# A gate in front of the second weight pool of a mixture of experts: its first load waits for a GpSimd memset that is queued behind the first gather

## The chip, the cores and the metric

The kernel runs on one core of a Trainium2 chip. The metric is the device time of one execution in microseconds. Before the change it is 1295.51 us, the median of 3 runs (1295.21 to 1295.92). A core has the engines PE (matmuls), DVE (vector), ACT (scalar), POOL (GpSimd) and SP (which issues most DMAs here), each with an instruction stream of its own that it works off in the order of the program.

## The reference

One decoder layer over 1024 tokens of 1024 values in float32: a token mixer (sliding-window attention beside a spatial gate), a cross-attention to 256 memory tokens, and a mixture of experts. The change lies in the last one:

```python
p_group = softmax(xf @ w_router_group); g_idx = argmax(p_group)            # one of 4 groups
local = take(xf @ w_router_expert, g_idx); top_logit, top_idx = top_k(local, 2)   # two of its 8 experts
gate = softmax(top_logit) * p_group[g_idx]
# for each of the 32 experts e, over the tokens that chose it:
hid = silu(xblk @ w1[e]) * (xblk @ w3[e])
y[token] += gate * (hid @ w2[e])
```

## The kernel before

The dense part (mixer, cross-attention) runs to about 676 us. The last half of the tokens is then routed (`route`, a chain of small DVE, POOL and PE work that ends in the table `idx`), and the rest of the span is the expert stage.

In the expert stage `main` runs 32 rounds, one for each expert, in the order 0, 8, 16, 24, 1, 9 and so on. For a round:

- POOL gathers up to 96 token rows of the normalised residual `xd` from DRAM into a tile `X` (an indirect DMA, `gather`, L1021). There are two `X` tiles; the first two gathers are issued ahead of the first round, the gather of round i+2 in round i.
- `columns` (L1038) turns `X` by eight PE transposes and splits it into `xh` (ACT) and `xl` (DVE): matmuls run in a rounded float32 format, three for each product (L114, L115, L116).
- The weights of an expert come in 12 tiles `ew` of 128x1024, 0.5 MB each, four for each of `w1`, `w3`, `w2`. Each tile is used in two halves: ACT casts a half to `hi` (L1049), DVE makes `lo` = weight - `hi` (L1050). `hi` and `lo` have five buffers each, so ACT can be five casts ahead of PE.
- `hidden`: 48 matmuls into two `h`; ACT's `g` (silu, L1066) and DVE's `g` follow. `turn`: four PE transposes of `g`, split into `hh` (ACT) and `hlo` (DVE). `output`: 24 matmuls into two `y`; ACT writes them to `B`, scaled by the gate (L1090, two instructions). Round i does the `output` of expert i-1.
- POOL adds `B` into the output rows in DRAM (`scatter`, L1027).

The weight tiles come from two pools, `raw` with 19 and `more` with 18 buffers, in turn: tiles 0 to 18 in `raw`, 19 to 36 in `more`, 37 again in `raw`. `stream` (L989) allocates a tile and issues its load on SP's queue (L998). The first 24 tiles (two experts) are streamed ahead: 19 while the dense part ends, since `raw` lies in memory that is free by then, and the last five by `run_all(units)` at L1336, as soon as the dense part's pools are closed and `more` exists. From the third expert on, a round's tiles are loaded from within `main`. A load waits for the buffer that it overwrites (DVE's `lo` of the tile that was in it).

In round 20 `counts` computes on DVE, between the weights' instructions, how many experts have more than 96 tokens (`cnt`, `no`, `noc`, `noi`); every engine reads `noi` into a register (L1164), SP in the midst of its loads.

The order in which each engine gets its instructions is not the order of the code: a scheduler sets it when the program is built, from priorities and its own estimate of times. It also decides which buffer a tile gets.

Of the kernel before, what the change touches and what calls it, by code (L numbers as in the profile page):

```python
# [821 lines left out]
class Moe:  # L822
# [166 lines left out]
    def stream(self, r, src):  # L989

        for i in range(3):
            r.append([])
            for u in range(4):
                k = self.turns % (self.nraw + self.nmore)
                self.turns += 1
                pool, n = ("raw", self.nraw) if k < self.nraw else ("more", self.nmore)
                w = self.L[pool].tile([P, 1024], F32, name="ew", bufs=n)
                self.nc.sync.dma_start(w, src(i, slice(u * 1024, (u + 1) * 1024)))  # L998
                r[i].append(w)
                yield  # L1000
# [91 lines left out]
    def order(self):  # L1092
        return [g * 8 + j for j in range(8) for g in range(4)]

    def main(self, xd, out, pre, rest):


        idx, tb, n = self.idx, self.tb, self.cap
        order = self.order()
        ix = lambda i: idx[:n, order[i]:order[i] + 1]  # L1100
        touch = []

        def ordered(ins, i):
            for j, o in touch:
                if order[j] // 8 != order[i] // 8:
                    self.tc.declare_no_dep(ins.ins, o.ins, reason="rows of tokens of another group")
            touch.append((i, ins))

        X, B = (lambda i: self.X[i % len(self.X)]), (lambda i: self.B[i % len(self.B)])
        get = lambda i: self.gather(X(i)[:n], ix(i), xd)  # L1110
        for i in range(len(self.X)):
            get(i)
        xc = self.columns(X(0), n)
        prev = None
        turned = []

        def between():
            run_all(rest)
            if prev:
                turned.append(self.turn(prev[3], n))  # L1120

        def finish():
            i, e, w, g = prev
            b = B(i)
            self.output(w, turned.pop() if turned else self.turn(g, n), b, tb[:, 0, e:e + 1], n)
            ordered(self.scatter(b[:n], ix(i), out), i)

        for i in range(NE):
            if i == 20:
                self.counts()  # L1130
            e = order[i]
            w = pre.pop(e) if e in pre else self.expert(e)
            if i + len(self.X) < NE:
                get(i + len(self.X))
            with self.tc.issue_after(self.ready.ins) if i == 0 else nullcontext():
                g = self.hidden(w, xc, tb[:, 1, e:e + 1], n, between)
            if i + 1 < NE:
                xc = self.columns(X(i + 1), n)
            if prev:
                finish()  # L1140
            prev = (i, e, w, g)
        finish()
# [80 lines left out]
def run_all(*gens):  # L1223
    for g in gens:
        for _ in g:
            pass


def to_tail(g):
    while next(g) != "tail":  # L1230
        pass


def interleave(a, b, ra, rb):

    live = [a, b]
    while live:
        for g, n in ((a, ra), (b, rb)):
            for _ in range(n):
                if g in live and next(g, live) is live:  # L1240
                    live.remove(g)


def dense(m):
    run_all(m.gate(0), m.gate(1))
    kv = m.kv()
    next(kv)
    interleave(kv, m.mix_tokens(), 1, 1)
    run_all(m.u(0), m.u(1))


def build(tc, a, dbg=None, cap=96):
    nc = tc.nc
    L = {}
    with ExitStack() as top:
        def pool(stack, name, **kw):
            L[name] = stack.enter_context(tc.tile_pool(name=name, bufs=1, reuse_waits="tile", **kw))

        pool(top, "const", side="left")
        L["dram"] = top.enter_context(tc.tile_pool(name="dram", bufs=1, space=DRAM))  # L1260
        xd = L["dram"].tile([T, D], F32, name="xd")
        m = Pre(tc, a, L, xd)
        m.rs2 = L["const"].tile([P, 8], F32, name="rs2")
        m.logit = L["const"].tile([P, 8, 36], F32, name="logit")
        m.setup()
        moe = Moe(tc, a, L, m, cap)
        moe.turns, moe.nraw, moe.nmore, moe.nhl = 0, 19, 18, 5
        pre = ExitStack()
        mix = ExitStack()
        for n in ("act", "ring", "half", "tmp"):  # L1270
            pool(pre, n, side="left")
        for n in ("early", "q2", "mem", "mix", "rt0"):
            pool(mix, n, side="right")
        pool(pre, "pt", side="left")
        pool(pre, "ps", space=PSUM)
        m.start(0, lambda: m.load(PIECES["q"][0], 0, 1))
        q = m.q()
        next(q)
        m.setup_mixer()
        interleave(q, m.x_stats(0), 1, 1)  # L1280
        run_all(m.mem_stats())
        m.use_stats()
        moe.consts()
        m.router_weights()
        dense(m)
        m.q_norm()
        mem = m.memory()
        at = m.attn()
        interleave(mem, at, 1, 1)
        run_all(mem)  # L1290
        run_all(m.x_stats(1))
        run_all(m.out_proj())
        x = m.cross()
        to_tail(x)
        m.start(1)
        m.use_stats()
        q = m.q()
        interleave(x, q, 1, 1)
        dense(m)
        m.q_norm()  # L1300
        co = m.co_proj(0)
        at = m.attn()
        interleave(at, co, 2, 1)
        run_all(co)
        interleave(m.out_proj(), chain([0], m.co_tail(0), moe.route(0)), 1, 1)
        x = m.cross()
        to_tail(x)
        next(x)
        co = m.co_proj(1, lambda: run_all(x))
        next(co)  # L1310
        next(co)
        mix.close()
        pool(top, "rt1", side="right")
        pool(top, "raw", side="right")
        pool(pre, "st", side="right")
        order = moe.order()
        ahead = {e: [] for e in order[:2]}
        units = chain(*(moe.ahead(e, r) for e, r in ahead.items()))
        for _ in range(6):
            next(units)  # L1320
        early = islice(units, moe.nraw - 6)
        interleave(co, early, 1, 1)
        run_all(co, early, m.co_tail(1))
        ro = moe.route(1)
        next(ro)
        next(ro)
        next(ro)
        if dbg == "size":
            for n, p in L.items():
                print(n, getattr(p, "current_size", lambda: 0)() / P)  # L1330
            return
        pre.close()
        for n in ("more", "ov", "rows", "ew", "hl"):
            pool(top, n, side="left")
        pool(top, "ps", space=PSUM)
        run_all(units)  # L1336
        moe.rows()
        moe.main(xd, a["out"], ahead, ro)
        moe.overflow(xd, a["out"])
        if dbg == "size2":  # L1340
            for n in L:
                print(n, getattr(L[n], "current_size", lambda: 0)() / P)
            return
        if dbg:
            dbg(nc, a, m, moe, xd)
# [69 lines left out]
```

## Time and profile before

| | |
|---|---|
| median of the runs | 1295.51 us |
| the profiled execution | 1300.52 us, its span 1298.8 us |
| busy shares of the span | PE 94%, DVE 77%, ACT 70%, POOL 15% |
| moved by DMA | 317.95 MB, mean 245 GB/s; SP's and ACT's queue 283.04 MB |
| mean granted clock of PE | 0.974 |
| what ACT's and DVE's work on `ew` waits for, whole span | ACT's casts 35.9 us (DVE), PE 12.2 us (ACT); no row names a load |

The profiled execution is 0.4% above the median of the others. Busy shares are means over stages with different limits, so the stretches are read one by one below. In the tables of stretches the number in brackets is the count of instructions, and the clock is the share of full speed that was granted.

### The profile page before, as it was taken

The page shows a single profiled execution, that of the slowest core. Times are in us where ns is not written, and L with a number is a line of the kernel's source. Part 1 is how long each engine was busy: PE and PEld are TensorE (multiplying, and loading weights), DVE is VectorE, ACT ScalarE, POOL GpSimd, SP SyncE. Part 2 cuts the span into 40 slices and gives each one's busy share as a digit, 9 for nine tenths or more (in the row PEclk, how much of TensorE's full clock was granted, in tenths as well). Part 3 has the DMA queues.
Part 4 walks back from the last instruction along what each step waited for, and adds up shares of the span by engine and source line. Part 5 has one row for each costly group of instructions (what it writes and reads, how often), then busy time and mean ns, then how long its engine had stood idle before and what let it go on. Part 6 is the DMA issues. An engine that isn't in the chain of part 4 may idle for free.

```text
span 1298.8 us, 19994 instructions
## 1 busy us (share of the span) xinstructions
PE 1226.2 (94%) x6514; PEld 963.0 (74%) x6514; DVE 1006.2 (77%) x1991; ACT 904.7 (70%) x1739; POOL 190.6 (15%) x229
## 2 busy tenths in 40 slices
PE   7999889998999998999994999999999999999995
PEld 5998878887899777788773677777777777766663
DVE  6568886556365999646546899999999999988884
ACT  6559663444366774444433999999999999988884
POOL 1312220011120112110004111111111111111100
PEclk9999999998999999999996999999999999999998
DMA  8436555335423345633599889999999959999981
GB/s 282 152 108 205 174 181 195 122 115 171 136 85 117 93 138 163 225 100 113 186 342 364 289 297 383 391 380 380 372 383 374 381 166 364 380 390 384 390 307 15
DMA packets 114603, 317.95 MB, mean 245 GB/s; under 512 B 13760, under 2 KB 33344, under 8 KB 114496
## 3 DMA queue, kind: packets, MB, share of 16 engines
q1 hardware_dynamic: 95280, 283.04, 60.2%
q0 software_dynamic: 10624, 29.38, 9.0%
q10 hardware_dynamic: 8592, 4.23, 1.1%
q8 instruction: 52, 0.85, 0.3%
q14 instruction: 55, 0.45, 0.1%
HBM read 293.52 MB, written 31.46 MB: 250 GB/s over the span
## 4 chain that ended last, share of the span: by engine, by line
issue 42%; PE 35%; DVE 9%; POOL 8%; ACT 3%; DMA 3%; POOLq 0%; SPq 0%; DVEq 0%; ACTq 0%
PE mm L114 8%; PE mm L116 8%; PE mm L115 8%; POOL out_dram L1027 3%; POOL X L1021 2%; DVE wlo L99 1%; DMA raw<-in_wp_dram 1%; DVE S L491 1%; PE sc L114 1%; PE sc L115 1%; PE tp L193 1%; PE sc L116 1%; DVE S L474 1%; DVE ptl L107 1%; PE av L114 1%
## 5 line engine op out<-in xcount | busy, mean ns | idle before, releaser
L1050 DVE TENSOR_TENSOR lo<-ew,hi 128x512 fp32r<-128x512 f32 x768 | 477.7, 685 | 37.8 <-ACT hi L1049 35.9
L1049 ACT CAST hi<-ew 128x512 fp32r<-128x512 f32 x768 | 446.1, 621 | 32.8 <-PE h L116 7.0
L115 PE MATMUL h<-lo,xh 128*96 128x512 f32 x512 | 204.2, 399 | 2.7 <-DVE lo L1050 2.6
L114 PE MATMUL h<-hi,xh 128*96 128x512 f32 x512 | 205.3, 401 | 0.2 <-ACT xh L106 0.2
L116 PE MATMUL h<-hi,xl 128*96 128x512 f32 x512 | 203.6, 398 | 0.3 <-DVE xl L107 0.3
L114 PE MATMUL mm<-ah,whi 128*128 128x512 f32 x416 | 166.7, 402 | 12.1 <-ACT whi L98 7.4
L98 ACT CAST whi<-raw 128x1024 fp32r<-128x1024 f32 x92 | 96.1, 1047 | 112.0 <-PE mm L115 54.4
L116 PE MATMUL mm<-ah,wlo 128*128 128x512 f32 x416 | 164.9, 396 | 0.6 <-DVE wlo L99 0.5
L115 PE MATMUL mm<-al,whi 128*128 128x512 f32 x416 | 164.9, 396 | 0.5 <-DVE al L107 0.5
L99 DVE TENSOR_TENSOR wlo<-raw,whi 128x1024 fp32r<-128x1024 f32 x92 | 112.7, 1226 | 66.9 <-ACT whi L98 66.9
L114 PE MATMUL mm<-whi,ah 128*128 128x256 f32 x448 | 129.1, 289 | 3.5 <-ACT t8b L409 2.1
L115 PE MATMUL mm<-wlo,ah 128*128 128x256 f32 x448 | 128.1, 287 | 0.0
L116 PE MATMUL mm<-whi,al 128*128 128x256 f32 x448 | 128.0, 286 | 0.0
L115 PEld LDWEIGHTS h<-lo,xh 128*96 128x96 f32 x512 | 83.5, 163 | 41.3 <-DVE lo L1050 6.9
L114 PEld LDWEIGHTS h<-hi,xh 128*96 128x96 f32 x512 | 83.4, 163 | 38.2 <-ACT hi L1049 4.9
L116 PEld LDWEIGHTS h<-hi,xl 128*96 128x96 f32 x512 | 83.4, 163 | 34.5 <-DVE xl L107 1.0
L114 PE MATMUL y<-hi,hh 128*96 128x512 f32 x256 | 100.3, 398 | 1.4 <-ACT hh L106 1.4
L115 PE MATMUL y<-lo,hh 128*96 128x512 f32 x256 | 101.0, 395 | 0.2 <-DVE lo L1050 0.2
L116 PE MATMUL y<-hi,hlo 128*96 128x512 f32 x256 | 100.5, 393 | 0.0
L114 PEld LDWEIGHTS mm<-ah,whi 128*128 128x128 f32 x416 | 79.0, 190 | 27.7 <-ACT whi L98 7.9
L116 PEld LDWEIGHTS mm<-ah,wlo 128*128 128x128 f32 x416 | 79.0, 190 | 17.7 <-DVE wlo L99 1.7
L115 PEld LDWEIGHTS mm<-al,whi 128*128 128x128 f32 x416 | 79.1, 190 | 16.0 <-DVE al L107 1.1
(315 smaller groups left out, 2077.1 us busy)
## 6 DMA issues: line engine op xcount, KB each, us to landing
ew<-in_wm_dram SPq DMA_DIRECT2D x384, 512.0 KB, 11.6
raw<-in_wp_dram SPq DMA_DIRECT2D x92, 512.0 KB, 4.2
xr<-in_xT_dram SPq DMA_DIRECT2D x24, 256.0 KB, 4.0
xr<-in_x_dram SPq DMA_DIRECT2D x16, 256.0 KB, 4.3
km<-md POOLq DMA_DIRECT2D x8, 512.0 KB, 4.0
x1d<-q SPq DMA_DIRECT2D x16, 256.0 KB, 2.4
xr<-x1d SPq DMA_DIRECT2D x16, 256.0 KB, 3.4
sq<-in_xT_dram SPq DMA_DIRECT2D x8, 256.0 KB, 5.3
```

Source lines behind the costliest of these rows:

```text
L98: nc.scalar.copy(hi[:, s], w[:, s])
L99: nc.vector.tensor_sub(lo[:, s], w[:, s], hi[:, s].bitcast(F32))
L107: nc.vector.tensor_sub(lo, src, hi.bitcast(F32))
L114: mm(out, ah, bh, start=start, stop=False)
L115: mm(out, ah, bl, start=False, stop=False)
L116: mm(out, al, bh, start=False, stop=stop)
L193: self.nc.tensor.matmul(pt[:, t:t + 1], src[:, t * P:(t + 1) * P], self.z[:, 0:1], start=True, stop=True)
L474: nc.vector.tensor_tensor_reduce(out=S[:, j, kc], in0=ps[:, i, kc], in1=self.mask[:, kc], scale=1.0, scalar=-3.0e38, op0=ALU.add, op1=ALU. ...
L1021: return self.nc.gpsimd.indirect_dma_start(out=x, out_offset=None, in_=src, in_offset=bass.IndirectOffsetOnAxis(ap=idx, axis=0), bounds_ch ...
L1027: return self.nc.gpsimd.indirect_dma_start(out=dst, out_offset=bass.IndirectOffsetOnAxis(ap=idx, axis=0), in_=x, in_offset=None, bounds_ch ...
L1049: nc.scalar.copy(hi, w)
L1050: nc.vector.tensor_sub(lo, w, hi.bitcast(F32))
```

## The change

`main` now gets `units`, the generator that streams the tiles still to be loaded ahead, and runs it after the first two gathers, instead of `build` running it before `main`. When the first tile of `more` is allocated, POOL writes four columns of it with a memset, which is to be issued after the first gather on POOL's queue (`issue_after` orders issue only; it does not wait for the gather to land). The load of this tile overwrites the memset's columns, so it waits for the memset.

```diff
     def stream(self, r, src):
...
                 w = self.L[pool].tile([P, 1024], F32, name="ew", bufs=n)
+                if pool == "more" and self.behind is not None:
+                    with self.tc.issue_after(self.behind.ins):
+                        self.nc.gpsimd.memset(w[:, :4], 0.0)
+                    self.behind = None
                 self.nc.sync.dma_start(w, src(i, slice(u * 1024, (u + 1) * 1024)))
...
-    def main(self, xd, out, pre, rest):
+    def main(self, xd, out, pre, rest, units):
...
-        for i in range(len(self.X)):
+
+        self.behind = get(0)
+        for i in range(1, len(self.X)):
             get(i)
+        run_all(units)
         xc = self.columns(X(0), n)
...
-        run_all(units)
         moe.rows()
-        moe.main(xd, a["out"], ahead, ro)
+        moe.main(xd, a["out"], ahead, ro, units)
```

The lines behind the edit move by 4 (L998 is L1002, L1049 is L1053, L1164 is L1171 in the changed kernel). The order of the instructions changes in three places.

The first is SP's queue where the loads of `raw` end. Before (`ew_7272` is tile 18, `ew_7408` tile 19):

```order
L998 DMA ew_7268<-in_wm_dram 128x1024 [waits DMAHW4_49]
L998 DMA ew_7270<-in_wm_dram 128x1024 [waits DMAHW6_49]
L998 DMA ew_7272<-in_wm_dram 128x1024 [waits DMAHW0_49]
L998 DMA ew_7408<-in_wm_dram 128x1024 [waits DMAHW3_49,PE_49]
L998 DMA ew_7410<-in_wm_dram 128x1024 [waits DMAHW4_49,DVE_49,PE_49]
L998 DMA ew_7412<-in_wm_dram 128x1024 [waits DMAHW6_49]
```

In the changed program (`ew_7272` is tile 18, `ew_8070` and `ew_8072` are tiles 37 and 38, `ew_7420` is tile 19, on which the memset is made):

```order
L1002 DMA ew_7268<-in_wm_dram 128x1024 [waits DMAHW4_49]
L1002 DMA ew_7270<-in_wm_dram 128x1024 [waits DMAHW6_49]
L1002 DMA ew_7272<-in_wm_dram 128x1024 [waits DMAHW0_49]
L1002 DMA ew_8070<-in_wm_dram 128x1024 [waits DMAHW7_49,DVE_49]
L1002 DMA ew_8072<-in_wm_dram 128x1024 [waits DMAHW0_49,DVE_49]
L1002 DMA ew_7420<-in_wm_dram 128x1024 [waits DMAHW1_49,PE_49,Pool_49]
L1002 DMA ew_7423<-in_wm_dram 128x1024 [waits DMAHW2_49,PE_49]
```

Tile 19's load now waits for POOL, and two later tiles stand ahead of it, which wait for DVE's `lo` of tiles 0 and 1. On POOL the memset stands right behind the second gather. From tile 39 on, each load waits for the same `lo` in both programs.

The second is ACT's order, from round 15 of the 32 on. Before, from the last casts of round 14 to near the end of round 15 (`hi`, `hh`, `g`, `xh` and `B` as above):

```order
L1049 CAST hi<-ew 128x512 x9
L106 CAST hh<-tp 128x384
L1066 ACTIVATE g<-h,tb 96x512
L1049 CAST hi<-ew 128x512 x8
L106 CAST xh<-tp 128x384 x2
L1049 CAST hi<-ew 128x512 x6
L1090 ACTIVATE B_7420<-y,tb 96x512
L1049 CAST hi<-ew 128x512
L1090 ACTIVATE B_7420<-y,tb 96x512
```

In the changed program, from within round 15 into round 16:

```order
L106 CAST hh<-tp 128x384
L1070 ACTIVATE g<-h,tb 96x512
L1053 CAST hi<-ew 128x512 x9
L106 CAST xh<-tp 128x384 x2
L1053 CAST hi<-ew 128x512 x5
L1094 ACTIVATE B_7410<-y,tb 96x512 x2
L1053 CAST hi<-ew 128x512 x4
L106 CAST hh<-tp 128x384
L1053 CAST hi<-ew 128x512 x4
L1070 ACTIVATE g<-h,tb 96x512
L1053 CAST hi<-ew 128x512 x9
```

The program before has the same second form too, from round 24 on; in the changed program it stands nine rounds earlier, in rounds 15 to 23 as well. On PE the eight transposes of `X` stand in one piece in the first form (48 `h` with four transposes of `g` in their middle, eight transposes, 24 `y`), and in four pieces of three, one, four and four (of `g`) in the second.

The third is where SP reads `noi`. Before, on SP:

```order
L85 DMA raw<-in_wp_dram 128x1024
L782 DMA xr<-x1d_5624 128x512
L998 DMA ew<-in_wm_dram 128x1024 x244
L1164 TENSOR_LOAD noi
L1164 ISA x2
L998 DMA ew<-in_wm_dram 128x1024 x127
```

In the changed program:

```order
L85 DMA raw<-in_wp_dram 128x1024
L782 DMA xr<-x1d_5624 128x512
L1002 DMA ew<-in_wm_dram 128x1024 x237
L1171 TENSOR_LOAD noi
L1171 ISA x2
L1002 DMA ew<-in_wm_dram 128x1024 x134
```

Thirteen more loads of `ew` stand ahead of these rows in both, so `noi` is read after 250 loads instead of 257. DVE, which makes `noi`, has it three `lo` earlier in the changed program (7 instead of 10 `lo` of that round ahead of it).

## Rows read from the trace of the kernel before

**Rows 1.** Busy time of each engine by stretch, then PE's clock, DMA share, GB/s

```profile
692.00:700.30 8.30, 0.01 (x1) 0.01 (x1) 4.71 (x19) 0.31 (x2) 4.12 (x6) 0.50 1.03 366
777.30:883.20 105.90, 105.90 (x506) 75.43 (x505) 101.27 (x169) 100.75 (x181) 14.51 (x12) 1.00 1.03 383
1149.30:1243.90 94.60, 92.57 (x422) 62.19 (x421) 83.83 (x141) 80.59 (x151) 12.29 (x9) 1.00 1.03 388
```

**Rows 2.** Waits of PE, 670 to 730 us: total, times, longest

```profile
PE tp L1038 <- DMA X<-xd,idx: 9.0, 1, 9.0
```

**Rows 3.** POOL in order of time, 689 to 705 us

```profile
692.43 1.30 POOL L1021 DMA_INDIRECT X<-xd,idx  x1 [1.41 <-issue]
694.03 1.34 POOL L1021 DMA_INDIRECT X<-xd,idx  x1 [0.30 <-issue]
696.49 1.47 POOL L976 TENSOR_TENSOR vg<-E,rb 128x128 bf16<-128x128 bf16 x4 [1.11 <-DVE rb L967]
```

**Rows 4.** Landing of the gather issued at 692.4 us

```profile
DMA to landing us min/median/max: 7.8/7.8/7.8
```

**Rows 5.** POOL in order of time, middle of the stage: two scatters

```profile
1022.74 1.44 POOL L1027 DMA_INDIRECT out_dram<-B,idx  x1 [5.69 <-ACT B L1090]
...
1040.39 1.44 POOL L1027 DMA_INDIRECT out_dram<-B,idx  x1 [5.69 <-ACT B L1090]
```

**Rows 6.** POOL in order of time, late in the stage: two scatters

```profile
1184.03 1.44 POOL L1027 DMA_INDIRECT out_dram<-B,idx  x1 [10.10 <-ACT B L1090]
...
1202.95 1.44 POOL L1027 DMA_INDIRECT out_dram<-B,idx  x1 [10.07 <-ACT B L1090]
```

**Rows 7.** All waits, 1149.3 to 1243.9 us (5 rounds)

```profile
ACT g L1066 <- PE h L116: 6.1, 5, 1.2
PEld h L115 <- DVE lo L1050: 5.0, 10, 0.6
```

**Rows 8.** Waits between compute engines, 777.3 to 883.2 us (6 rounds): the only row

```profile
DVE lo L1050 <- ACT hi L1049: 4.1, 12, 0.4
```

**Rows 9.** Work on the weight tiles, 630 to 767.3 us: duration min, median, max

```profile
L1049 ACT CAST hi<-ew x83: 607/622/632, 683.9 to 766.6; 128x512 fp32r<-128x512 f32 x83
...
L998 SPq DMA_DIRECT2D ew<-in_wm_dram x70: 327/328/914, 632.2 to 756.2; - x70
```

**Rows 10.** Work on the weight tiles, 670.5 to 695.4 us

```profile
L998 SPq DMA_DIRECT2D ew<-in_wm_dram x18: 327/418/914, 670.7 to 694.7; - x18
...
L1050 DVE TENSOR_TENSOR lo<-ew,hi x5: 681/682/683, 691.5 to 693.9; 128x512 fp32r<-128x512 f32 x5
```

**Rows 11.** Landing of the gather issued at 720.5 us

```profile
DMA to landing us min/median/max: 5.5/5.5/5.5
```

**Rows 12.** Landing of the last scatter, issued at 1285.3 us

```profile
DMA to landing us min/median/max: 4.3/4.3/4.3
```

**Rows 13.** DMA queues, 696.5 to 700.3 us: packets, MB, share of 16 engines

```profile
q1 hardware_dynamic: 250, 0.90, 71.6%
q0 software_dynamic: 156, 0.38, 32.6%
```

**Rows 14.** Waits of SP's queue, 745 to 772 us

```profile
SPq L998 <- DVE lo L1050: 22.7, 11, 10.7
```

**Rows 15.** Waits of SP's queue, 1036 to 1080 us

```profile
SPq L1164 <- DVE xl L107: 25.3, 1, 25.3
```

**Rows 16.** DVE in order of time, around 1070 us

```profile
1069.97 0.13 DVE L1163 CAST noi<-noc 128x1 int32<-128x1 f32 x1
```

**Rows 17.** Work on the weight tiles, 630 to 1070.9 us

```profile
L1049 ACT CAST hi<-ew x495: 607/622/635, 683.9 to 1070.5; 128x512 fp32r<-128x512 f32 x165
L1050 DVE TENSOR_TENSOR lo<-ew,hi x491: 674/684/804, 691.5 to 1070.5; 128x512 fp32r<-128x512 f32 x164
L998 SPq DMA_DIRECT2D ew<-in_wm_dram x257: 327/328/1197, 632.2 to 1045.0; - x129
```

**Rows 18.** Landing of the load issued at 1071.0 us

```profile
DMA to landing us min/median/max: 5.4/5.4/5.4
```

## Prediction

> **What bounds the kernel now.** I read the page first: its shares of busy time (the table above) say that most of the span is one matmul behind another, so a change can only act where PE stands idle or where its pace is set by somebody else. The view by stretches then shows the two places that matter here. Between 692.0 and 700.3 us PE does nothing and its granted clock is 0.50, while the DMA engines are full [rows 1]. The waits of PE say what for: one wait of 9.0 us for the landing of the first gather, `X<-xd,idx` [rows 2]. That gather is issued at 692.43 [rows 3] and lands 7.8 us later [rows 4]. From there on the kernel is 32 rounds, one for each expert, and in them PE is busy all the time, but with ACT at 100.75 and DVE at 101.27 of 105.90 us [rows 1]: three engines are almost equally loaded, and the order in which ACT and DVE take their work sets PE's pace. The scatters, one for each round, show that pace. In the middle they follow each other by 1040.39 - 1022.74 = 17.65 us [rows 5]; late in the stage by 1202.95 - 1184.03 = 18.92 us [rows 6]. The two waits views of those stretches name the difference: late, ACT's `g` waits 6.1 us in 5 rounds, 1.2 us in each, for PE's last `h` matmul, with the casts of the next weights queued behind it; in the middle no such row stands, and the only wait among the compute engines is DVE's for the casts [rows 7, 8].
>
> The weight loads are not what PE waits for. When load 70 is about to be issued, at 767.3, 83 casts (two to a tile) have begun, so the loads are 70 - 41 = 29 tiles ahead, and a round uses 12 tiles [rows 9].
>
> **The change part by part.** *The gate.* Before, 18 loads (tiles 19 to 36) are issued between 670.7 and 694.7 [rows 10]. Now tile 19's load waits for a memset of 128x4 on GpSimd, which stands behind both gathers. The second gather's issue ends at 694.03 + 1.34 = 695.4 [rows 3], so the gate opens near 695.5. Behind tile 19's load in SP's queue stand tiles 20 to 36 and everything after them; ahead of it the order now has the loads of tiles 37 and 38, which wait only for DVE's `lo` of tiles 0 and 1. DVE makes its first five `lo` from 691.5 on [rows 10], so these two loads go out at about 693 and 694, beside the gather. The memset delays nothing on GpSimd: the multiply behind it waits for DVE until 696.49 [rows 3].
>
> *What the gate returns.* The idle engine waits for one landing, so the gain is what the gather becomes shorter. Before, it takes 7.8 us among full queues [rows 4]. The nearest row for less traffic is the gather at 720.5, with one or two loads beside it: 5.5 us [rows 11]. A scatter of the same 393 KB at the very end, with nothing beside it, takes 4.3 us [rows 12]. So the gain is between nothing (7.8 again) and 3.5 us. I take 5.5, since two loads of 0.5 MB are beside it here too: **-2.3 us**.
>
> In the stretch in which the gather's packets move, its queue took 32.6% and the loads' queue 71.6% of the engines [rows 13]: it was not stuck behind all that SP had queued, it had a share throughout. The Trainium skill (DMA: Bandwidth & Descriptors, Queues, rings and completion order) says that each DMA engine goes round its queue rows packet by packet, which agrees with that and speaks against this change: clearing SP's queue can only give back the other queue's turns. The packets move for 3.8 us; by that rule halving this is an estimate of 1.9 us of gain, and the sum would be 0.4 us higher than mine.
>
> *The 18 loads that come later.* Cover: the lead. With 18 loads of 0.524 MB at the 383 GB/s of the full stretch [rows 1], 1.37 us each, tile 36 lands at about 695.5 + 5 + 25 = 725. Its first cast is the 73rd, and at 767.3 the 83rd has begun [rows 9], ten casts or 10/24 of a round earlier is 760. So 35 us remain. The deficit doesn't last either: load 70 waits for DVE in one wait of 10.7 us [rows 14], in both programs for the same `lo`, so the lead is cut to the same 29 tiles before and after. Cost: 0. If that cover were gone, 18 x 1.37 = 25 us would be late, and it would show as casts that wait for loads.
>
> *What the build did with it.* The order of the program is made at build time by a scheduler with its own estimate of times, and the later loads change its choice far from the edit. ACT's order in a round exists in two forms. In the first, `hh` and `g` stand together after nine casts, and the two `B` have a cast between them; in the second the two `B` stand together, `hh` comes after four casts and `g` after four more. Before, the second form begins in the round of expert 24 of the order; in the changed program it begins in that of expert 15. That is nine rounds more. PE's transposes go with it: eight in one place in the first form, four pieces in the second. The first form has 17.65 us to a round and the second 18.92 [rows 5, 6], and the second's extra wait of 1.2 us on ACT [rows 7] cannot be made up by an engine that is busy 95% of the round. 9 x (18.92 - 17.65) = **+11.4 us**. Bounds: 0, if the second form is slow for another reason than its order; 13, if the counting instructions that DVE has between the rounds 19 and 20, hidden before, now add one wait more.
>
> *SP's wait for the count.* SP reads `noi` in the middle of its loads. Before, it has issued 257 loads by then, waits 25.3 us [rows 15], and reads when DVE has made `noi` at 1069.97 [rows 16]; at 1070.9, 495 casts have begun and 491 `lo` [rows 17]. The next load lands 5.4 us after its issue [rows 18]. So the loads were 257 - 247 = 10 tiles ahead at the worst point. Now SP stands there after 250 loads, and DVE makes `noi` three `lo` earlier, that is, at about 487 `lo` and 490 to 492 casts. Tile 250's first cast is the 501st: 9 to 11 casts of 18.92/24 = 0.79 us, 7 to 8.5 us, against 1 us to the issue and 5.4 to the landing. That is 1 to 2 us of lead, and after it 12 loads take 12 x 1.37 = 16.4 us and the gather's and scatter's share, against 18.92 for their use, so it grows. I put **+0.4 us** on it; bounds 0 and 4.
>
> **The sum.** -2.3 + 11.4 + 0.4 = +9.5 us. The profiled execution took 1300.52 us, of which the span is 1298.8; so profiled I expect 1310.0. The median of the runs, 1295.51, is 5.0 us below the profiled one, a difference of level that I carry over: 1295.5 + 9.5 = **1305.0 us**.
>
> **The rivals.**
> 1. *The gain alone, faster.* The second form costs nothing by itself: its 18.92 us come from what else is there after 1149 (a lead of few tiles since SP's wait, DMA share 1.03 [rows 1]). Then earlier rounds in this form run at 17.65 and only the gather counts: 1295.5 - 2.3 = 1293.2, 1292.0 at best. For it: before, the second form occurs only after SP's wait. Against it: the DMA share is 1.03 also in the stretch at 17.65 [rows 1], and the waits name ACT, PE and DVE, no load [rows 7]. It decides if ACT's `g` does not wait in the rounds 16 to 24. Chance 0.08.
> 2. *The loads become the bound after SP's wait.* The lead there is gone instead of 1 to 2 us; each load that is late moves ACT's cast and, since `hi` and `lo` have five buffers each, PE. 2 to 5 us more: 1307 to 1310. For it: my lead is smaller than the spread of the landings. Against it: the loads catch up by about 1 us in a round. Chance 0.17.
> 3. *The gate does nothing, and the order still costs.* The two loads that slip ahead and the second gather fill the engines, and the gather takes 7.8 us again: 1307.3. Chance 0.07.
> 4. *A DMA-bound stage.* The share of 1.03 [rows 1] means that every idle microsecond before 695 is paid at the end. Held loads of 25 us, less what the gather leaves, some 15 us on top of the order: 1315 and more. Against it the 29 tiles [rows 9] and the common wait of load 70. Chance 0.03.
>
> **How the numbers follow.** My forecast has 0.65: between 1303 and 1306.5, from -3.5 to -1.3 on the gather, +10.5 to +12 on the order, 0 to 2 on SP's wait. With rivals 2 and 3 the slower side reaches 1310. The range that leaves out no more than 2 in 10 goes from 1300.0, which a second form at half its price gives (1295.5 - 1.5 + 5.7), to 1310.0. A measurement of this kernel can tell about 0.2%, 2.6 us, from no change. Faster than 1292.9 needs rival 1 with its best gain, 0.04; within 0.2% is the rest of rival 1 and some mixtures, 0.06; slower 0.90.
>
> **What would show it.** In the profile after: the first gather lands in 5 to 6 us, and PE's wait for it is about 6.7 us instead of 9.0; SP's load of tile 19 starts near 695.5, with two loads at 693 and 694 ahead of it; the scatters follow each other by 17.65 us up to that of round 13 and by 18.9 from round 14 on; ACT's `g` waits 1.2 us in some 15 rounds; no cast waits for a load before SP's wait, and after it at most by a few us. I am wrong if the rounds 16 to 24 run at 17.65 us, or if casts wait for loads in many rounds.

## The result and the profile after

The changed kernel takes 1307.84 us (median of 4 runs, 1307.12 to 1308.34), the kernel before 1295.72 us on the same chip. The ratio is 1.0082, 95% interval 1.0067 to 1.0098: slower by 8.7 to 12.7 us. The profiled execution took 1308.34 us, its span is 1306.6 us.

The rows that answer to the ones of before, from the trace of the changed kernel. Lines have moved: the load L998 is L1002, the cast L1049 is L1053, the gather L1021 is L1025, the scatter L1027 is L1031, ACT's `g` L1066 is L1070, the read of `noi` L1164 is L1171. First the gate, in the view of POOL in order of time (it answers to [rows 3]):

```profile
690.88 1.30 POOL L1025 DMA_INDIRECT X<-xd,idx  x1 [1.41 <-issue]
692.49 1.35 POOL L1025 DMA_INDIRECT X<-xd,idx  x1 [0.30 <-issue]
693.83 0.12 POOL L1000 MEMSET ew<- 128x4 f32 x1
```

The memset of 0.12 us stands behind the second gather. Both gathers are 1.55 us earlier than in [rows 3], and the first load of `ew` is 2.0 us earlier (630.2 against 632.2 us). That is not the gate's doing: DVE's `idx`, on which the gathers wait, starts between 685.8 and 691.5 us in the thirteen profiled executions of this study, and from the first load to `idx` it is 58.1 to 59.7 us both with a gate and without. So times are counted from `idx` below: from its start to the end of the span it is 1298.8 - 691.35 = 607.45 us before and 1306.6 - 689.79 = 616.8 us after, **+9.4 us**.

PE's waits, 670 to 730 us (answers to [rows 2]: 9.0 us):

```profile
PE tp L1042 <- DMA X<-xd,idx: 5.9, 1, 5.9
```

The stretches of [rows 1], in the changed kernel (same columns):

```profile
690.00:696.00 6.00, 0.33 (x2) 0.33 (x3) 5.17 (x19) 0.31 (x2) 3.83 (x6) 0.50 0.59 187
...
777.00:883.00 106.00, 106.00 (x506) 75.52 (x505) 101.37 (x169) 100.86 (x181) 14.52 (x12) 1.00 1.03 386
1083.00:1178.00 95.00, 92.89 (x423) 62.38 (x422) 84.10 (x142) 80.51 (x150) 13.68 (x10) 1.00 1.03 386
```

The DMA engines now have room while the gather is under way (0.59 where it was 1.03). The middle is as before, and the third row, 66 us earlier than the third of [rows 1], already looks like it: ACT at 80.5 of 95 us.

Scatters, POOL in order of time (answers to [rows 5, 6]):

```profile
945.74 1.44 POOL L1031 DMA_INDIRECT out_dram<-B,idx  x1 [5.69 <-ACT B L1094]
...
963.39 1.44 POOL L1031 DMA_INDIRECT out_dram<-B,idx  x1 [5.69 <-ACT B L1094]
980.64 1.44 POOL L1031 DMA_INDIRECT out_dram<-B,idx  x1 [5.29 <-ACT B L1094]
...
1056.44 1.44 POOL L1031 DMA_INDIRECT out_dram<-B,idx  x1 [10.11 <-ACT B L1094]
1078.13 1.44 POOL L1031 DMA_INDIRECT out_dram<-B,idx  x1 [14.31 <-ACT B L1094]
...
1135.00 1.44 POOL L1031 DMA_INDIRECT out_dram<-B,idx  x1 [10.09 <-ACT B L1094]
1153.92 1.44 POOL L1031 DMA_INDIRECT out_dram<-B,idx  x1 [10.08 <-ACT B L1094]
```

Up to that of round 13 (963.39) the scatters follow each other by 17.65 us; after one round of 17.25 us, from that of round 14 (980.64) to that of round 29, by 18.92 to 18.97 us, but for one gap, from round 18 to 19, which is 1078.13 - 1056.44 = 21.69 us. Waits in 1083 to 1178 us, and in 1056.4 to 1079.5 us, the round of that gap (first rows answer to [rows 7]):

```profile
ACT g L1070 <- PE h L116: 6.2, 5, 1.2
PEld h L115 <- DVE lo L1054: 4.7, 9, 0.6
...
ACT hi L1053 <- DMA ew<-in_wm_dram: 3.5, 1, 3.5
...
PE h L114 <- ACT hi L1053: 1.7, 1, 1.7
```

The gap is a cast that waits 3.5 us for a load, which no cast did in the kernel before. SP's queue tells why, 1030 to 1090 us (answers to [rows 15]):

```profile
SPq L1171 <- DVE noi L1170: 29.1, 1, 29.1
```

From the first scatter to the last the accounts are: round 13 to round 31 takes 1293.14 - 963.39 = 329.75 us, before 315.57, so +14.2. The gap is 2.7 over its neighbours, where counting cost 0.3 before: **+2.4**. The rest, **+11.8**, is nine more rounds at the slower pace. From `idx` to the first scatter it is 44.1 in place of 49.0: **-4.9**. The sum is +9.3 of the +9.4.

### The profile page after: what moved, and what is told of

It is laid out like the page before. It is cut to its first block, busy times and chain, and to the rows that moved or that the text cites. A ratio compares the mean times of both kernels' runs of the same rounds, so it can differ in the third digit from the quotient of the medians.

```text
span 1306.6 us, 20006 instructions
## 1 busy us (share of the span) xinstructions
PE 1230.8 (94%) x6514; PEld 957.4 (73%) x6514; DVE 1005.8 (77%) x1991; ACT 899.0 (69%) x1739; POOL 193.0 (15%) x230
## 4 chain that ended last, share of the span: by engine, by line
issue 41%; PE 33%; DVE 9%; POOL 8%; DMA 5%; ACT 4%; POOLq 0%; SPq 0%; DVEq 0%; ACTq 0%
PE mm L114 8%; PE mm L115 8%; PE mm L116 8%; POOL out_dram L1031 4%; POOL X L1025 2%; DVE wlo L99 1%; DMA raw<-in_wp_dram 1%; DVE S L491 1%; PE sc L115 1%; PE sc L114 1%; PE sc L116 1%; PE tp L193 1%; DMA ew<-in_wm_dram 1%; DVE ptl L107 1%; DVE S L474 1%
## 5 line engine op out<-in xcount | busy, mean ns | idle before, releaser
L1053 ACT CAST hi<-ew 128x512 fp32r<-128x512 f32 x768 | 438.3, 622 | 31.7 <-PE y L116 7.8
L114 PE MATMUL mm<-ah,whi 128*128 128x512 f32 x416 | 166.3, 401 | 12.1 <-ACT whi L98 6.9
L116 PEld LDWEIGHTS mm<-ah,wlo 128*128 128x128 f32 x416 | 78.7, 189 | 17.5 <-DVE wlo L99 1.7
```

The source lines that it names most:

```text
L114: mm(out, ah, bh, start=start, stop=False)
L116: mm(out, al, bh, start=False, stop=stop)
L1053: nc.scalar.copy(hi, w)
```

## The experiments

First and second order are the prediction's first and second form. Theory A is the one of the prediction: the order of the instructions on ACT, DVE and PE costs 1.28 us in each of nine more rounds, SP's earlier stand for the count a little, and the gate itself gives something ahead of round 0. The rivals are that the late loads make the order slow (B, C), that the gate gives nothing (D), that counting itself makes the gap (E), and that the loads cannot follow a faster pace (F). To move an order without the gate, edges were added at build time (issue order on one engine, no wait) from each instruction of a round to its neighbours; the heart of the helper is

```
+        def pin(line, base, slots):
+            for k, xs in slots:
+                seq = [line[base + k - 1]] + xs + [line[base + k]]
+                for a, b in zip(seq, seq[1:]):
+                    after(b, a)
...
```

where `line` is all casts of ACT, all `lo` of DVE or all matmuls of PE, and a slot (k, xs) puts `xs` behind the k-th of them in a round. Where PE is bound, all its matmuls of these rounds are also chained one behind the other. Each run's ratio is to runs of the kernel before on its own chip, and the runs come from several chips: compare ratios, or times counted from `idx`, rather than medians.

| run | median us | ratio, 95% interval | `idx` to first scatter, us | `idx` to end, us |
|---|---|---|---|---|
| before | 1295.7 | 1 | 49.0 | 607.5 |
| changed | 1307.8 | 1.0082 (1.0067 to 1.0098) | 44.1 | 616.8 |
| e1_order2_no_gate | 1325.1 | 1.0214 (1.0192 to 1.0236) | 48.5 | 634.1 |
| e2_gate_order1 | 1297.9 | 1.0011 (0.9997 to 1.0025) | 45.8 | 608.6 |
| e3_count_early | 1305.9 | 1.0069 (1.0049 to 1.0090) | 44.5 | 614.9 |
| e4_gate_order1_all | 1291.2 | 0.9960 (0.9944 to 0.9977) | 44.2 | 600.5 |
| e5_order2_exact | 1314.3 | 1.0123 (1.0098 to 1.0147) | 48.9 | 625.2 |
| e6_gate_order1_read | 1286.2 | 0.9907 (0.9888 to 0.9925) | 44.2 | 594.8 |
| e7_nogate_order1_read | 1287.8 | 0.9923 (0.9902 to 0.9945) | 47.4 | 598.0 |
| e8_g_later | 1298.8 | 1.0008 (0.9994 to 1.0021) | 44.7 | 608.4 |
| e9_act_only_order1 | 1286.8 | 0.9923 (0.9908 to 0.9939) | 45.8 | 598.2 |
| e10_move_only | 1296.4 | 1.0001 (0.9987 to 1.0016) | 49.4 | 608.2 |
| e11_hold_two_more | 1284.2 | 0.9903 (0.9888 to 0.9919) | 42.3 | 593.0 |

**e10: the call moved, no memset.**

```
-        self.behind = get(0)
+        self.behind = None
+        get(0)
```

> The changed kernel without the memset, so that no load waits for a gather; only the call that issues the loads stands behind the gathers in the program. The engines' late order is then that of the kernel before, and SP reads the count after 257 loads. Theory A: nothing of the loss and nothing of the gain comes from the move, so as before, within 1 us, with the first gather landing in 7.5 to 7.9 us. Rival I, the move by itself changes the stage: more than 3 us to either side.

```profile
PE tp L1042 <- DMA X<-xd,idx: 9.4, 1, 9.4
```

The time is that of before, PE waits 9.4 us for the gather, and the second order begins where it did before. So the move of the call is nothing; the memset, and the loads it holds, bring both the gain and the other order.

**e1 and e5: the second order without the gate.** The lines are those of e5; in e1 they begin with i = 16.

```
+        for i in range(15, 31):
+            act = [(-2, self.hhs[i - 1:i]), (2, self.gs[i:i + 1]), (11, self.xhs[2 * i + 2:2 * i + 4]),
+                   (18, self.bs2[2 * i - 2:2 * i])]
+            dve = [(-2, self.hls[i - 1:i]), (10, self.gv[i:i + 1]), (10, self.xls[2 * i + 2:2 * i + 4])]
+            pe = [(-16, self.tg[4 * i - 4:4 * i] + self.tx[8 * i + 8:8 * i + 12]), (19, self.tx[8 * i + 12:8 * i + 15]),
+                  (31, self.tx[8 * i + 15:8 * i + 16])]
```

> The kernel before, without gate or memset, with ACT, DVE and PE bound at build time to the second order from round 15 on, as the changed kernel has it (SP reads the count after 255 loads). Theory A, the order itself costs 1.28 us per round: eight or nine more rounds, 10.2 to 11.5 us, so about 1306 us, and scatters that follow each other by 18.9 us from round 15 on. Rival B, the second order is only slow because of what the gate did to the loads: no change, 1295.5 us, and 17.65 us up to round 23.

It was slower than either theory said: 19.84 us a round. The binding had put PE's matmuls for `y` in the order in which they are written, and the changed kernel's order is not that one: there three products of `hi` with `hh` go ahead, each of the two products (`lo` with `hh`, `hi` with `hlo`) that are written before them. So this run is no test of A; e5 binds that turn too (`y` in the order 0 to 6, 9, 7, 8, 12, 10, 11, 15, 13, 14, 16 to 23).

> The kernel before, without gate or memset, with ACT, DVE and PE bound at build time to the changed kernel's order from round 15 on, now also in the turn of PE's matmuls for y (SP reads the count after 254 loads). Theory A: 18.93 us from scatter to scatter from round 15 on, 1.28 us more in nine or ten rounds than before, 11.5 to 13 us, so 1307 to 1309 us. Rival B, the gate's late loads make the order slow: 17.65 us up to round 23 and 1296 us. If the 19.85 us of the first such run come from the turn of y, they are gone; if not, they stay and the time is 1325 again.

Scatters and waits (1100 to 1156 us) of e5:

```profile
1103.54 1.44 POOL L1026 DMA_INDIRECT out_dram<-B,idx  x1 [10.11 <-ACT B L1095]
1122.47 1.44 POOL L1026 DMA_INDIRECT out_dram<-B,idx  x1 [10.08 <-ACT B L1095]
...
ACT g L1068 <- PE h L115: 3.7, 3, 1.2
```

18.93 us, and 1.2 us of `g` in each of three rounds: the changed kernel's stage, in a kernel that holds no load back. From the scatter of round 14 to that of round 28 every round takes 18.93 to 18.99 us but that of the count. B is out. The time is some 6 us over the forecast, and one round accounts for most of it, that of the count, 24.57 us, where bound instructions of PE and ACT stand behind the counting ones on DVE (waits of 2.4 and 4.0 us); in the kernel before, the count costs 0.3 us, so this belongs to the binding. The run also leaves the difference of e1 to the turn of the `y` matmuls: 0.9 us a round.

**e2: the first order with the gate.** The same helper, rounds 10 to 24, with

```
+            act = [(5, self.hhs[i - 1:i]), (5, self.gs[i:i + 1]), (13, self.xhs[2 * i + 2:2 * i + 4]),
+                   (19, self.bs2[2 * i - 2:2 * i - 1]), (20, self.bs2[2 * i - 1:2 * i])]
+            dve = [(5, self.hls[i - 1:i]), (12, self.gv[i:i + 1]), (12, self.xls[2 * i + 2:2 * i + 4])]
+            pe = [(24, self.tg[4 * i - 4:4 * i]), (48, self.tx[8 * i + 8:8 * i + 16])]
```

> The changed kernel, gate and memset as they are, with the three engines bound to the first order up to round 24, as the kernel before has it (SP still reads the count after 250 loads). Theory A: the gate gives 3 to 5 us and SP's earlier stand costs 2.7, so 1293 to 1295 us, and 17.65 us from scatter to scatter up to round 18. Rival C, the held loads cost something themselves through the stage: 17.9 us or more in the rounds 14 to 23, and over 1300 us. Rival D, the gate gives nothing: 1298 us.

Of the loss 8 us are gone, and the rounds up to 17 take 17.65 us: C is out. But nothing is gained either. From `idx` to the first scatter it is 3.2 us shorter than before, so D is out; around the count, from the scatter of round 17 to that of round 20, it takes 17.94 + 22.35 + 17.30 us, 4.6 over the pace, where before it took 0.3 over it. There, from 1045 to 1092 us, casts wait for loads:

```profile
ACT hi L1054 <- DMA ew<-in_wm_dram: 4.7, 2, 3.1
```

With the faster order SP's earlier stand costs 4.3 us, not 2.4, and that eats the gate's gain.

**e3: the count earlier.**

```
-            if i == 20:
+            if i == 8:
```

> The changed kernel with the count taken in round 8 in place of round 20, so that SP reads it after 116 loads; the order of the engines in the late rounds stays the second one. Theory A: the one gap of 21.7 us between two scatters goes back to 18.9, so 2.7 us less than the changed kernel, 1305 us. Rival E, the gap is a matter of the counting instructions on DVE and not of late loads: it moves to round 8 and the time stays at 1307.8.

The gap is gone (18.96 us from round 18 to 19), and round 8 has none of its size (18.53 + 17.07 us): the gap was late loads, E is out.

**e4: the first order in all rounds, the count in round 8.** As e2 with rounds 10 to 30, and the edit of e3.

> The changed kernel with the first order bound in all rounds up to 30 and the count taken in round 8. Theory A: the gate's 3 to 5 us, and 1.28 us in each of the seven rounds in which the kernel before has the second order, so 1295.5 - 4 - 9 = 1282 us. Rival B: the late rounds keep 18.9 us whatever the order, 1291 us. Rival F, the loads cannot follow at 17.65 us to a round in the late stage (12 loads of 1.37 us and gather and scatter beside them): waits of casts for loads, 1286 to 1291 us.

Rival F's figure, or so it looked: 17.65 us up to round 20, then rounds of up to 20.1 among such of 17.65, and casts wait for loads again (waits, 1080 to 1260 us):

```profile
ACT hi L1054 <- DMA ew<-in_wm_dram: 7.1, 11, 1.3
```

The theory that came of it (G in e6's expectation): the DMA engines are full, a round's 12 loads, the gather and the scatter take a little over 17.65 us, and the stage lives on the lead with which it starts. What breaks it is SP's stand, 22.7 us here, in which no load is issued.

**e6: count and read apart.** As e4, and SP reads later in its queue:

```
             if i == 8:
                 self.counts()
+            if i == 12:
+                self.read()
```

> The changed kernel with the first order in all rounds up to 30, the count computed in round 8 and read by SP in its place among the loads of round 12, so that SP need not wait for it. Theory G, what the loads lack late is the lead that SP's wait took: without that wait the lead falls by 0.4 tiles in a round, from 29 to about 17, no cast waits for a load, 17.65 us to the last rounds, 1284 us. Rival F, the loads are too slow for 17.65 us by themselves: casts wait for loads from round 21 on as before, 1290 us.

Loads issued and casts begun up to 1180 us, first in e4, then in e6:

```profile
L1001 SPq DMA_DIRECT2D ew<-in_wm_dram x333: 327/328/926, 629.6 to 1178.6; - x167
L1054 ACT CAST hi<-ew x648: 607/622/637, 680.5 to 1179.8; 128x512 fp32r<-128x512 f32 x162
```

```profile
L1001 SPq DMA_DIRECT2D ew<-in_wm_dram x344: 327/328/637, 630.1 to 1179.9; - x172
L1054 ACT CAST hi<-ew x653: 607/622/636, 682.4 to 1180.0; 128x512 fp32r<-128x512 f32 x164
```

The lead is 333 - 324 = 9 tiles in e4 and 344 - 326.5 = 17.5 in e6 (two casts to a tile). No cast of e6 waits for a load, and from round 9 to round 28 the scatters follow each other by 17.65 us:

```profile
1122.79 1.44 POOL L1030 DMA_INDIRECT out_dram<-B,idx  x1 [5.69 <-ACT B L1099]
...
1140.44 1.44 POOL L1030 DMA_INDIRECT out_dram<-B,idx  x1 [5.69 <-ACT B L1099]
```

The lead falls from 29.5 tiles at 820 us (111 loads, 163 casts) by 12 in 20 rounds, 0.6 a round where 0.4 was expected, and still lasts. Seven slow rounds of the kernel before are gone with it: 1286.2 us, 0.9907 of the kernel before on its chip, and so faster than both kernels.

**e7: e6 without the gate.** (`run_all(units)` where the kernel before has it, no memset.)

> The same without gate and memset (the units where the kernel before has them). Theory A: slower than with the gate by what the gate gives ahead of round 0, 3 to 5 us, 1288 us, with the same 17.65 us in the rounds. Rival C, the gate's gain is given back later as the held loads are missing: no difference between the two within 1 us.

Counted from `idx`, e7 takes 598.0 us and e6 594.8: the gate is worth 3.2 us here, 3.2 of them ahead of the first scatter, and nothing is given back. The medians differ by only 1.7 us, and the intervals of the two ratios overlap, so the times alone do not show the 3.2. The runs of e7 fall into two groups (1286.8 to 1287.8 and 1291.2 to 1291.3) and those of e6 don't; what comes ahead of `idx` varies by that much from one execution to the next, but that this makes the groups isn't shown.

**e8: `g` alone.**

```
+                if i and k == 4:
+                    late = self.cast
...
-        nc.scalar.activation(g[:n], ps[0][:n], AF.Silu, scale=rs[:n])
+        with self.tc.issue_after(late.ins):
+            nc.scalar.activation(g[:n], ps[0][:n], AF.Silu, scale=rs[:n])
```

> The changed kernel, and in it only ACT's g bound behind the fifth cast of the second half of the round, four casts later than in the second order and as in the first; the transposes on PE and the two B stay as the second order has them. Theory A as the prediction put it, the cost is ACT in line behind PE's last h matmul: its 1.2 us are gone, 17.7 to 18.0 us in the rounds 15 to 30, 1292 to 1297 us. Rival H, the cost is in PE's scattered transposes or in B: 18.9 us stay, 1307 us.

Scatters and the waits of ACT and DVE in three rounds (1100 to 1156 us):

```profile
1109.25 1.44 POOL L1031 DMA_INDIRECT out_dram<-B,idx  x1 [9.56 <-ACT B L1097]
1127.64 1.44 POOL L1031 DMA_INDIRECT out_dram<-B,idx  x1 [7.08 <-ACT B L1097]
...
DVE g L1074 <- PE h L116: 2.0, 3, 0.7
...
ACT xh L106 <- PE h L115: 1.6, 3, 0.5
ACT B L1097 <- PE y L116: 1.4, 3, 0.5
ACT hi L1053 <- PE y L116: 1.2, 3, 0.4
```

Between the two: ACT's wait of 1.2 us for `g` is gone entirely, and the round takes 18.4 us, so 0.54 of the 1.28 are back and 0.75 are not yet. The prediction named the longest wait; three shorter ones of ACT, 0.4 to 0.5 us each, stand in the same rounds.

**e9: the first order on ACT alone.** As e6, with only the list `act` kept of the three.

> As e6, but only ACT is bound to the first order in the rounds 10 to 30; PE and DVE stand as the build then puts them (PE's transposes of X in pieces, as in the second order, from round 15 on). Theory A: ACT's order is what counts, so 17.65 us to the last rounds and 1286 us. Rival H, PE's scattered transposes carry the rest that e8 left (18.41 against 17.65 us): 18.1 to 18.4 us in the rounds 16 to 30, 1294 to 1298 us.

```profile
1105.49 1.44 POOL L1031 DMA_INDIRECT out_dram<-B,idx  x1 [8.07 <-ACT B L1096]
1123.19 1.44 POOL L1031 DMA_INDIRECT out_dram<-B,idx  x1 [8.08 <-ACT B L1096]
```

17.70 us, with PE's transposes of X still in pieces (three, one and four). H is out for what e8 left: the places on PE are worth 0.05 us of the 1.28, and ACT's order as a whole the rest. DVE is not told apart from ACT by this run: bound nowhere, it moved along (five `lo` between its `hlo` and its `g`, where the second order has twelve and the first seven). How the 0.7 beside `g` divide among `xh`, `hh` and the two `B` wasn't tried.

**e11: two more loads held.** On e6, so that the loads of tiles 37 and 38 queue behind those of the gate:

```
+                with self.tc.issue_after(self.prior.ins) if self.turns in (38, 39) else nullcontext():
+                    self.prior = self.nc.sync.dma_start(w, src(i, slice(u * 1024, (u + 1) * 1024)))
```

> As e6, and the two loads that slip ahead of the gate (tiles 37 and 38) are queued behind the held ones. If the loads beside the gather set its time, it lands in 4.3 to 4.8 us in place of 5.0 to 5.3, and idx to the first scatter takes 0.3 to 0.7 us less than the 44.2 of e6, about 1285.5 us. Rival D', the rest of the gather's time is its own: no change, 44.2 us and 1286.2.

PE's wait for the gather, in e11:

```profile
PE tp L1042 <- DMA X<-xd,idx: 4.7, 1, 4.7
```

In e6 it is 6.4 us. So two loads beside the gather cost 1.7 us, more than forecast, and from `idx` to the end it is 593.0 us against 594.8, the shortest of all. By the ratios, 0.9903 and 0.9907 on two chips, the two can't be told apart.

## Why the prediction was right, step by step

**What carries it** is the nine rounds, and it was right in place and size: +11.4 forecast, +11.8 in the accounts; e5 shows the cost without a gate, e2 the gate without the cost. What the prediction gave as the cause is less than half of it. It put the 1.28 us on ACT's `g` behind PE's last `h`; by e8 `g` alone is 0.54. By e9 it is ACT's order as a whole, 1.25, with `xh`, `hh` and `B` early as well, and with DVE's places as they follow from it.

**The gate's return** was mis-sized, and the step is the one that read the queues' shares. The prediction took the gather's queue to have a share throughout, since it had 32.6% in the stretch in which its packets move [rows 13]. By microsecond, before (issue at 692.4) and in e11 (issue at 692.5), packets, MB, share:

```profile
q1 hardware_dynamic: 115, 0.41, 102.8%
...
q1 hardware_dynamic: 95, 0.34, 86.2%
q0 software_dynamic: 14, 0.06, 14.9%
```

```profile
q0 software_dynamic: 98, 0.19, 70.5%
```

Before, the microsecond from 695.4 (first row) holds loads alone, and the gather's first packets show in the one from 696.4, 4 us after the issue; in e11 they show from 694.5 on, 2 us after it. So with loads in flight the first packet comes 2 us later, and the gather's queue then has 14.9% in its first microsecond instead of 70.5%. The estimate by the Trainium skill (DMA: Bandwidth & Descriptors, Queues, rings and completion order), turns packet by packet and so 1.9 us from halving the moving time, fell short of all that was measured: 3.1 us with two loads left beside the gather, and 4.7 with none (9.4 in e10, 4.7 in e11). These waits vary from one execution to the next: 8.7 to 9.4 us in the five kernels without a gate, 5.9 to 6.4 in the seven with two loads beside the gather. Between the bounds 0 and 3.5 I took 2.3; the gather gave **3.1**.

**A term that I didn't have** is the rest of the 4.9 us ahead of the first scatter. PE's granted clock, in the kernel before and in the changed one (windows, clock third from the end):

```profile
706.30:712.40 6.10, 4.59 (x23) 2.96 (x22) 4.20 (x6) 4.06 (x7) 2.29 (x5) 1.00 1.03 375
712.40:716.50 4.10, 3.65 (x12) 2.56 (x12) 2.06 (x5) 1.52 (x3) 0.40 (x2) 0.59 0.84 300
```

```profile
701.80:707.80 6.00, 4.04 (x21) 2.59 (x20) 4.19 (x6) 3.72 (x6) 2.69 (x6) 1.00 1.03 369
707.80:711.90 4.10, 4.10 (x21) 2.98 (x21) 2.48 (x5) 3.05 (x4) 0.00 (x0) 1.00 1.02 407
```

Before, the clock comes up to the higher level (1.00, 2.4 GHz), falls again to the lower one (0.50, 1.2 GHz) for most of 4.1 us, in which 12 matmuls are done, and comes up for good. After, it doesn't fall again, and the same 4.1 us hold 21. In the stretch ahead of it PE stands idle once, in both kernels alike, waiting for POOL's `vg`, the end of the routing (PE in order of time, before and after):

```profile
712.85 0.55 PE L979 MATMUL tp<-vg,S 128*128 128x192 bf16 x4 [1.96 <-POOL vg L976]
```

```profile
707.76 0.49 PE L979 MATMUL tp<-vg,S 128*128 128x192 bf16 x4 [1.96 <-POOL vg L976]
```

All thirteen traces have this idle time, 1.94 to 1.96 us of it. In the six in which it begins 4.6 to 4.9 us after the clock came up, the clock falls at its end or up to 0.3 us later; in the seven in which it begins 5.2 to 5.9 us after, the clock stays up. The fall isn't the gate's alone: it falls again in before, e1, e5 and e10, not in e7, of those without a gate, and in e2 and e9, not in the changed kernel, e3, e4, e6, e8 and e11, of those with one. With like compared to like, the gate gives 45.8 against 48.5 to 49.4 us where the clock falls, and 44.1 to 44.7 (e11 apart) against 47.4 where it doesn't: 3.1 to 3.2 by the means. The second fall itself is 1.1 to 2.0 us more, so the changed kernel's profiled execution got some 1.7 us that may not come each time.

**SP's wait for the count** was the step that failed, +0.4 forecast and +2.4 found, 4.3 where the rounds are fast (e2). SP stands there after 250 loads as forecast, and up to 1066.6 us, when `noi` is read, 491 casts have begun in the trace, as forecast. Wrong was which tile comes next. I let casts take tiles in the order of loading, so that tile 250 is due with the 501st cast. But an expert's last four tiles, `w2`, are used a round later than they are loaded: tiles 248 to 251 are those of round 20's `w2`, used in round 21, and the tile due first is 252, the first of round 21's `w1`, at cast 24 x 21 - 8 + 1 = 497, six casts away and two loads further down the queue. The trace agrees: ACT has begun 496 casts when it stops, and the third load behind SP's stand, issued at 1068.7 us, is the one that lets it go on:

```profile
1075.55 1.14 ACT L1053 CAST hi<-ew 128x512 fp32r<-128x512 f32 x2 [3.55 <-DMA ew<-in_wm_dram]
```

Six casts at 0.79 us are 4.7 us, against 1 us to the issue and 5.4 to the landing: 1.7 us late, and with up to 1.37 us for each of the two loads ahead up to 4.4. The trace has 3.5. Rival 2 described it, with 2 to 5 us, and the measured 1307.84 us lies in its band (1307 to 1310) and above the one that the forecast had for itself (1303 to 1306.5).

**The held loads** cost nothing by themselves: in the three traces with a gate and the count in round 20, two casts (0.3 us each) and three `lo` (0.4 us each) wait for a load ahead of SP's stand. Rival 4 was right in one thing: from the gate on the DMA engines are full (1.03 in the stretches shown), and the lead with which the stage starts is spent, not renewed, at the fast pace (e6). By that loss of 0.6 of 12 tiles in 17.65 us, a round's loads with its gather and scatter take some 18.6 us, an estimate; the prediction counted 16.4 us and the shares of the other two, and let the lead grow. A spent lead becomes time only where something takes the rest of the lead at once.

**The level.** I carried over 5.0 us between the profiled execution and the runs. The traces show differences of that size ahead of `idx`, which is at 691.35 us in that execution and down to 685.8 in others, with a gate and without; that the 5.0 us are of this kind isn't shown, as the other executions of the kernel before left no trace. By the traces, counted from `idx`, the change costs 9.4 us where the sum said 9.5; in it, 2.0 too little for SP's wait and 0.4 for the order stand against 0.8 too little for the gather and the 1.7 of the clock. That the sum comes out to 0.1 us is luck: errors of 2.4 us on one side met 2.5 on the other, and one of them is a clock that falls in one execution and not in the next. By the medians it is 12.1, with the interval of 8.7 to 12.7, so the forecast of 1305.0 is 2.8 us under the 1307.84; what is ahead of `idx` moves by more than that from one execution to the next.

## What to carry to other kernels

A wait added in one place is priced twice: for what it holds, and for what the build makes of the later instructions. Compare the order on every engine before and after; here the held loads gave 3.1 us, and a turned order that begins some 290 us later took 11.8. Where ACT, DVE and PE are equally loaded, bind the order that is known to be good rather than leave it to an estimate of times (e6 keeps the gate's gain and takes back seven rounds that were slow already). And where one queue issues all loads, a read in it that waits for a late value spends the whole lead: compute the value early and read it several rounds further down.

## What the runs showed of the hardware

A gather issued while loads fill the engines gets its first packet 4 us after its issue, and 2 us with none in flight; two loads issued beside it cost 1.7 of the 4.7 us that it saves when alone. The granted clock can fall a second time, 6.8 us after it rose, with PE busy but for one idle time of 1.95 us (4.59 us busy of 6.10 ahead of the fall, 4.04 of 6.00 where it did not come): in the six traces with the fall that idle time begins 4.6 to 4.9 us after the rise, in the seven without it 5.2 to 5.9 us after. No run moved that idle time by itself, so that its place decides is a reading and not shown; kernels with a gate and without show both. And the turn of three of PE's matmuls for `y` was worth 0.9 us a round (e1 against e5).
